# Attention in a hybrid decoder layer: values as the weights of a half-width product, two token tiles streamed, sums divided behind it

## The chip, the core and the metric

The kernel runs on one core of a Trainium2 chip. The metric is device time in microseconds for one execution. A core has five engines that work from queues of their own, in order: TensorE (PE, with its weight loads shown apart as PEld), VectorE (DVE), ScalarE (ACT), GpSimd (POOL) and SyncE (SP), which here issues most DMAs. Products land in PSUM, eight banks of 2 KB on each of 128 partitions; the other engines read them from there. Everything else lives in SBUF or DRAM.

## What is computed

One decoder layer on 1024 tokens of width 1024, float32. The part that matters here is the attention group, 8 heads of 64, and what follows it:

```python
z = h @ W_in                       # q, k, v of the attention, and the RWKV group's columns
# A: causal dilated window attention, branches (128,1), (512,4), (2048,16);
#    the branches share their scores, so that each key has a weight 0 to 3
#    num = sum_j count(t,j) exp(s_tj) v_j ;  den = sum_j count(t,j) exp(s_tj)
attn  = rms_norm(num / den, attn_out_gain)
rw    = rwkv7(...)                 # the recurrent group, R
mixed = concatenate([attn, rw]) @ w_out
x = x + rms_norm(mixed, norm_mix_post)
x = x + rms_norm(relu(rms_norm(x) @ w_ffn_up)**2 @ w_ffn_down)
```

The number of branches in which a key takes part is put into the scores as a logarithm, from a table `strip` that depends on the distance alone.

## The kernel before

The stages follow one another: norm of x and its transposes, the projections with the recurrent part (up to about 446 us), attention (462 to 637), the mixing with `w_out` (to about 758), and the two products of the feed-forward part, each by a Strassen-like scheme of seven products. Most products are fp32r with high and low parts (`mm3`, three products); `mm` with plain float32 operands leaves two records in the trace.

**Attention** (`attn_pair`, L837) goes over four pairs of heads, a pair holding two heads in 64 partitions each. For each head, `qr` is loaded twice into the two halves of the partitions (L842), GpSimd makes `qs` from it, rounded to fp32r and scaled (L844), and VectorE puts the remainder into the lower half (L845); so one product over 128 rows takes high and low part at once. `kr` is loaded in the same way (L850), GpSimd rounds it to `kh` (L853), VectorE forms the rest `kl` (L854). The raw tiles, `qs`, `kh` and `kl` have two buffers each, one for each head of a pair, so that the next pair's can be made when the present pair's last readers are done. `vT` is transposed by TensorE into `Vt` (L863), keys on the partitions.

Then eight tiles of 128 queries, i = 0 to 7, in two groups of four (`qg`). For a tile and a head the scores `pS` of all keys up to the diagonal are formed in banks of up to 512 columns (L888). VectorE adds the table and takes the minimum in one instruction (L890); ScalarE makes the exponential and its row sum `den` (L893). TensorE transposes the 128x128 blocks into `pT` (L900), and ScalarE (first bank) or VectorE (second bank) copies them into `PT` (L902, L904), keys on the partitions. The product `av` (L869 to L872) takes each block of `PT` as the weights and streams the 64 columns of the head's values:

```python
mm(po[:, ii, h], PTs[h][:, j], Vt[:, j, h * 64:h * 64 + 64], j == 0, j == i)
```

Its output has queries on the partitions, so the division by the row sum is one VectorE product with the reciprocal (L910, L912). It is emitted one tile late (`pend`). `ao` goes to DRAM as rows (`a_d`, L914); its squares are summed over the columns (L917, L918) for the RMS norm.

The order of the instructions of an engine comes from a scheduler that goes by the priority under which they were written. Attention is written with a high priority (L936, L1049); what remains of the projections (`rest`, the last pair's q, k and v), the loading of `w_out` (`load_wo`) and R's first products fill the gaps. In the recurrent part and, from L1078 on, in the mixing, TensorE's order is the written one (`manual_schedule`).

**The mixing** takes the token tiles in the order 0, 4, 1, 5, 2, 6, 3, 7. `half_a` (L975) loads 128 rows of `a_d`, scales them by the attention's RMS factor `sa[:, 1]` on ScalarE, transposes them (`half_t`, L961) and splits them into high and low part; `half_r` does the same without scale for R's rows. `half_mm` multiplies a half with four blocks of `w_out`, 24 products of 512 columns into `pm`. For the first two tiles R's half is done during the attention and kept in SBUF (`part`); R's half of the third is bound to come behind the last `av` (L1062). `mix_x1` (L988) adds the halves if they are apart, forms the squares and the norm and adds x.

The squares' sums `sq4` become `sa` by one reduction and the `rsqrt` chain on VectorE (L1064 to L1066).

## Time and profile before

| what | value |
|---|---|
| time, median of three runs | 1360.32 us (1360.21 to 1365.02) |
| the profiled execution | 1361.23 us; its span 1359.4 us |
| TensorE's granted clock, mean over the span | 0.991 |
| stage up to 70 us: length, PE, DVE, ACT busy | 70, 54.3, 54.8, 49.4 us |
| 70 to 446, projections and recurrence | 376, 362.1, 231.2, 149.8 us |
| 637 to 758, the mixing | 121, 114.7, 97.9, 69.6 us |
| 758 to 1056, up product | 298, 296.8, 218.0, 124.1 us |
| 1056 to the end, down product | 304, 292.8, 194.4, 123.3 us |

The span is the time from the first to the last instruction of the program; some 1.8 us of the execution lie around it. Busy time is the union of an engine's instructions. A matmul's record lasts until its last result is written, and records overlap, so that the price of one in a burst is read from the distance between the starts, not from its duration. In rows of the timeline the columns are start, length, engine, line, operation, output and inputs, weights' shape, streamed shape and count; neighbouring equal instructions are merged into one row. In rows of groups the columns are count, busy us, mean ns of one, and the idle time of the engine just before them with what ended it.

### The profile page before, as it was taken

To read this page: it belongs to the slowest core of one execution; us is meant where nothing else is said; L and a number is where in the kernel's file an instruction comes from. 1 tells how busy PE (TensorE), PEld (TensorE's weight loads), DVE (VectorE), ACT (ScalarE), POOL (GpSimd) and SP (SyncE) were. 2 spreads that over 40 slices of the span, in tenths; PEclk is the share of its full clock that TensorE was granted. 3 is DMA by queue.
4 is the path that set the end of the run, shared out by engine and by line. 5 is a ranking of instruction groups with operands and counts; after the bars stand their busy time and mean duration, and the time that the engine had idled before them with its cause. 6 is when DMAs were issued, how large, how long until landed. Compare 5 with 4: busy or idle time off the path is not lost.

```text
span 1359.4 us, 22401 instructions
## 1 busy us (share of the span) xinstructions
PE 1307.3 (96%) x8784; PEld 1086.4 (80%) x8784; DVE 914.7 (67%) x1647; ACT 625.0 (46%) x1026; POOL 44.7 (3%) x56
## 2 busy tenths in 40 slices
PE   6999999999999999999998999999999999999997
PEld 5777887788777798988887888888887888888885
DVE  7867658531678567655788986677766786445686
ACT  7652324233555367654656444343434344443442
POOL 0000000000000100110000000000000002000110
PEclk9999999899999999999999999999999999999999
DMA  7346746676685656321434344444366995346564
GB/s 255 114 170 163 194 125 179 184 206 204 182 248 145 194 145 181 102 55 38 138 121 139 132 168 152 168 153 150 132 209 217 322 349 172 95 139 200 186 215 157
DMA packets 161193, 231.02 MB, mean 170 GB/s; under 512 B 51680, under 2 KB 88800, under 8 KB 161088
## 3 DMA queue, kind: packets, MB, share of 16 engines
q1 hardware_dynamic: 153024, 208.62, 48.8%
q10 hardware_dynamic: 8064, 20.98, 4.6%
q8 instruction: 69, 1.13, 0.4%
q14 instruction: 36, 0.29, 0.1%
HBM read 156.66 MB, written 72.89 MB: 169 GB/s over the span
## 4 chain that ended last, share of the span: by engine, by line
PE 77%; DVE 11%; DMA 5%; ACT 4%; issue 2%; SPq 0%; POOL 0%; DVEq 0%; ACTq 0%; POOLq 0%
PE X L47 12%; PE dX L47 9%; PE Z L47 6%; PE pm L47 5%; PE dZ L47 5%; PE po L47 5%; PE dY L47 3%; PE z_av L47 3%; PE z_k L47 3%; PE Y L47 3%; PE pS L47 3%; PE z_v L47 3%; PE z_aq L47 2%; PE pT L900 2%; PE z_r L47 2%
## 5 line engine op out<-in xcount | busy, mean ns | idle before, releaser
L47 PE MATMUL dX<-wow,wou 128*128 128x512 f32 x768 | 176.6, 390 | 3.3 <-ACT wow L1106 1.8
L47 PEld LDWEIGHTS dX<-wow,wou 128*128 128x128 f32 x768 | 143.6, 188 | 35.6 <-DVE wow L1107 3.4
L47 PE MATMUL dZ<-wow,wou 128*128 128x512 f32 x384 | 87.4, 389 | 0.0
L47 PEld LDWEIGHTS dZ<-wow,wou 128*128 128x128 f32 x384 | 72.1, 188 | 14.9
L1106 ACT ACTIVATE wow<-wd 128x1024 fp32r<-128x1024 f32 x40 | 42.3, 1059 | 87.1 <-PE dZ L47 29.8
L1107 DVE TENSOR_TENSOR wou<-ur,wou 128x1024 fp32r<-128x1024 f32 x56 | 72.0, 1288 | 10.8 <-ACT wou L1106 10.5
L47 PEld LDWEIGHTS po<-Vt,PT 128*128 128x128 f32 x576 | 72.6, 191 | 4.8 <-ACT PT L902 2.2
L47 PE MATMUL po<-Vt,PT 128*128 128x64 f32 x576 | 74.0, 269 | 0.7 <-ACT PT L902 0.4
L1107 DVE TENSOR_TENSOR wow<-wd,wow 128x1024 fp32r<-128x1024 f32 x40 | 49.9, 1251 | 36.3 <-ACT wow L1106 35.8
L1106 ACT ACTIVATE wou<-ur 128x1024 fp32r<-128x1024 f32 x56 | 58.6, 1049 | 26.2 <-DMA ur<-u_d 18.8
L893 ACT ACTIVATE S<-S,mn 128x128 f32<-128x128 f32 (+7 forms) x64 | 49.4, 774 | 20.8 <-DVE mn L890 20.7
L890 DVE CUSTOM_DVE_ANT_0 S<-pS,stripT 128x512 f32<-128x512 f32 (+3 forms) x64 | 37.4, 590 | 26.1 <-PE pS L47 15.9
L1193 ACT ACTIVATE r<-u 128x512 f32<-128x512 f32 x48 | 30.1, 627 | 48.4 <-DVE u L1191 48.1
L47 PE MATMUL z_aq<-hT,wh_aq 128*128 128x512 f32 x128 | 47.3, 424 | 3.5 <-DVE ev_v L192 3.5
L47 PE MATMUL pm<-WO,mxr 128*128 128x512 f32 x192 | 48.6, 398 | 0.0
L902 ACT ACTIVATE PT<-pT 128x512 f32<-128x512 f32 (+3 forms) x64 | 32.9, 515 | 32.2 <-PE pT L900 30.2
L1107 DVE TENSOR_TENSOR wow<-TK,wow 128x1024 fp32r<-128x1024 f32 x16 | 20.8, 1301 | 38.9 <-ACT wow L1106 38.9
L47 PE MATMUL Z<-HB,wo 128*128 128x512 f32 x192 | 46.1, 389 | 0.0
L47 PE MATMUL pm<-WO,mxa 128*128 128x512 f32 x192 | 45.8, 394 | 0.0
L900 PE MATMUL pT<-cst,S 128*128 128x128 f32 x288 | 44.4, 276 | 1.0 <-DVE rden L910 0.5
L47 PE MATMUL X<-HB,wo 128*128 128x512 f32 x180 | 43.6, 390 | 1.6 <-ACT HB L1029 1.6
L47 PE MATMUL z_k<-hT,wh_k 128*128 128x512 f32 x128 | 43.2, 398 | 1.7 <-DVE z L223 1.4
(388 smaller groups left out, 3102.5 us busy)
## 6 DMA issues: line engine op xcount, KB each, us to landing
ur<-u_d SPq DMA_DIRECT2D x56, 512.0 KB, 4.2
wd<-in_wdown_dram SPq DMA_DIRECT2D x40, 512.0 KB, 3.9
u_d<-S SPq DMA_DIRECT2D x64, 256.0 KB, 2.1
u_d<-u SPq DMA_DIRECT2D x48, 256.0 KB, 2.1
wr_upa<-in_wup_dram SPq DMA_DIRECT2D x16, 512.0 KB, 3.8
wr_upb<-in_wup_dram SPq DMA_DIRECT2D x16, 512.0 KB, 3.8
TK<-in_wdown_dram SPq DMA_DIRECT2D x16, 512.0 KB, 7.3
x<-in_x_dram SPq DMA_DIRECT2D x8, 512.0 KB, 6.0
```

The source lines that it names most:

```text
L47: return PE.matmul(o, lhsT, rhs, start=start, stop=stop, skip_group_check=True)
L890: V.tensor_tensor_reduce(Sx[:, lo:hi], pS[:, :hi - lo], stripT[:, so:so + hi - lo], 1.0, 3e38 if k == 0 else mn[:, 0:1], OP.add, OP.min, a ...
L893: A.activation(Sx[:, :w], Sx[:, :w], AF.Exp, scale=-1.0, bias=mn[:, nbk - 1:nbk], accum_out=den[:, i, h:h + 1])
L900: PE.transpose(pt[:, j], Sx[:, (4 * k + j) * P:(4 * k + j + 1) * P], ident)
L902: A.activation(PT[:, 0:nb_], pt[:, 0:nb_], AF.Copy)
L1106: A.activation(w[:, 0, 0:n], raw, AF.Copy)
L1107: E.tensor_tensor(w[:, 1, 0:n], raw, w[:, 0, 0:n].bitcast(F32), OP.subtract)
L1193: A.activation(r, src, AF.Relu)
```

## The change

The product of probabilities and values is turned round. The 64 columns of a head's values become the weights, and the transposed probabilities of two query tiles (i = 2g and 2g+1, 256 columns, the later tile first) are streamed. The output has the head's 64 columns on the partitions, the first head on 0 to 63 and the second on 64 to 127, and the tokens along the columns. The two heads' products alternate. There are four groups g for each pair in place of two; `PT` holds two tiles of a head, block by block.

Since the queries are no longer on the partitions, the row sums can't divide by a scalar for each partition. Their reciprocals `rden` are written to DRAM (`rd_d`), loaded back spread over 64 partitions for each head (`rb`), and `ao` is the product of `po` and `rb`. `a_d` holds the attention output transposed, and `half_a` loads what it needs without a transpose; it splits the unscaled values, and the RMS factor moves behind the product: R's part is multiplied by its inverse (`sa[:, 2]`) ahead of the transposes where both halves are accumulated together, and the sum is scaled afterwards (`joint`), or, for the first two tiles, the attention half alone where the halves are added. The squares are summed over the pairs in `sqa` and over the partitions by eight products with two columns, ones in either half (`pq`).

The scores are the same products, but written for both heads of a tile ahead of their exponentials; the score tiles `S` have two buffers of 512 columns and two of 1024. For tiles 0 to 3 the second head's blocks are copied by VectorE instead of ScalarE. `qs` and `kh` are made on ScalarE instead of GpSimd. The evacuated projections and `ao` share two buffers `ev` in the attention's pool; before, the projections had three in a pool of their own. R's half of the third tile is no longer done behind the last `av` but in the mixing's loop.

The diff, without what the functions above show as removed:

```diff
-        a_d = dp.tile([S, 512], F32, name="a_d")
+        a_d = dp.tile([P, 4, S], F32, name="a_d")
+        rd_d = dp.tile([4, 4, 2, 2, P], F32, name="rd_d")
...
-                zt_ = evp.tile([P, 512], F32, name=f"ev_{nm}_{hf}", tag="ev" if i >= 8 else "kr", bufs=3 if i >= 8 else 8)
+                zt_ = evp.tile([P, 512], F32, name=f"ev_{nm}_{hf}", tag="ev" if i >= 8 else "kr", bufs=evb[0] if i >= 8 else 8)
...
-        ev_ctx = tc.tile_pool(name="ev2", bufs=2)
-        evp = ev_ctx.__enter__()
...
-        ap_ = at_ctx.__enter__()
-        sq4 = cp.tile([P, 4, 8], F32, name="sq4")
-        sa = cp.tile([P, 5, 8], F32, name="sa")[:, 0:2]
+        ap_ = evp = at_ctx.__enter__()
+        evb[0] = 2
+        sa = cp.tile([P, 9, 8], F32, name="sa")[:, 0:4]
         stripT = ap_.tile([P, S], F32, name="stripT", bufs=1)
+        sqa = ap_.tile([P, S], F32, name="sqa", bufs=1)
...
-                G.tensor_scalar(qs, qr, -0.125, 0.0, op0=OP.mult, op1=OP.add)
+                A.activation(qs, qr, AF.Copy, scale=-0.125)
...
-                gcopy(kh, kr)
+                A.activation(kh, kr, AF.Copy)
...
-            den = sm.tile([P, 8, 2], F32, name=f"den{p}", tag="den")
-            rden = sm.tile([P, 8, 2], F32, name=f"rden{p}", tag="rden")
...
+            def av(g, PTs, rb):
...
+                po = ps.tile([P, 512], F32, name=f"po{p}_{g}", tag="by"[g % 2], bufs=1)[:, 0:256]
+                for j in [0, 2 * g + 1] + list(range(1, 2 * g + 1)):
+                    n = 128 if j > 2 * g else 256
+                    for h in range(2):
+                        last_av[0] = mm(po[own[h], 0:n], Vt[:, j, h * 64:h * 64 + 64], PTs[h][:, 256 * j:256 * j + n], j == 0, j == 2 * g or g == 0)
+                cols = slice(256 * g, 256 * g + 256)
+                ao = ap_.tile([P, 512], F32, name=f"ao{p}_{g}", tag="ev")[:, 0:256]
+                V.tensor_tensor(ao, po, rb, OP.mult)
+                nc.sync.dma_start(a_d[:, p, cols], ao)
+                if p == 0:
+                    A.activation(sqa[:, cols], ao, AF.Square)
+                else:
+                    sq = ap_.tile([P, 256], F32, name=f"sqa{p}_{g}", tag="sq", bufs=1)
+                    A.activation(sq, ao, AF.Square)
+                    V.tensor_tensor(sqa[:, cols], sqa[:, cols], sq, OP.add)
...
             pend = []
...
-            def av(po, i, ii, PTs):
-                for h in range(2):
-                    for j in range(i + 1):
-                        last_av[0] = mm(po[:, ii, h], PTs[h][:, j], Vt[:, j, h * 64:h * 64 + 64], j == 0, j == i)
...
+            for g in range(4):
+                PTs = [ap_.tile([P, 1920 if g % 2 else 1408], F32, name=f"PT{p}_{g}_{h}", tag=f"PT{g % 2}") for h in range(2)]
+                den = sm.tile([P, 8, 2], F32, name=f"den{p}_{g}", tag="den")[:, 0:2]
+                for i in (2 * g, 2 * g + 1):
                     w = P * (i + 1)
...
+                    nbk = 1 if w <= 512 else 2
+                    Sx = [ap_.tile([P, 512 * nbk], F32, name=f"S{p}_{i}_{h}", tag=f"S{nbk}") for h in range(2)]
+                    mn = [sm.tile([P, 2], F32, name=f"mn{p}_{i}_{h}", tag="mn", bufs=4) for h in range(2)]
+                    for k in range(nbk):
+                        lo_, hi_ = 512 * k, min(w, 512 * k + 512)
+                        so = S - w + lo_
+                        pS = [ps.tile([P, 512], F32, name=f"pS{p}_{i}_{h}_{k}", tag="w") for h in range(2)]
+                        for h in range(2):
+                            for q in range(2):
+                                mm(pS[h][:, :hi_ - lo_], QS[h][:, i * P:(i + 1) * P], (KH, KL)[q][h][:, lo_:hi_], q == 0, q == 1)
+                        for h in range(2):
+                            V.tensor_tensor_reduce(Sx[h][:, lo_:hi_], pS[h][:, :hi_ - lo_], stripT[:, so:so + hi_ - lo_], 1.0,
+                                                   3e38 if k == 0 else mn[h][:, 0:1], OP.add, OP.min,
+                                                   accum_out=mn[h][:, k:k + 1])
                     for h in range(2):
...
+                        A.activation(Sx[h][:, :w], Sx[h][:, :w], AF.Exp, scale=-1.0, bias=mn[h][:, nbk - 1:nbk],
+                                     accum_out=den[:, h, 1 - i % 2:2 - i % 2])
+                        o = P * (2 * g + 1 - i)
                         for k in range(nbk):
                             nb_ = min(4, i + 1 - 4 * k)
                             pt = ps.tile([P, 4, P], F32, name=f"pT{p}_{i}_{h}_{k}", tag="ac"[k], bufs=1)
                             for j in range(nb_):
...
+                                PE.transpose(pt[:, j], Sx[h][:, (4 * k + j) * P:(4 * k + j + 1) * P], ident)
+                            f = (4 * k + nb_ - 1) * 256 + o
+                            dst = PTs[h][:, 4 * k * 256 + o:f + P] if nb_ == 1 else PTs[h].rearrange("p (j c) -> p j c", c=P)[:, (4 * k * 256 + o) // P:f // P + 1:2]
+                            if k == 0 and (h == 0 or nbk == 2):
+                                A.activation(dst, pt[:, 0:nb_], AF.Copy)
                             else:
...
+                                V.tensor_copy(dst, pt[:, 0:nb_])
+                    if i % 2 == 0 and pend:
+                        av(*pend.pop(0))
+                rden = sm.tile([P, 8, 2], F32, name=f"rden{p}_{g}", tag="rden")[:, 0:2]
+                V.reciprocal(rden, den)
+                nc.sync.dma_start(rd_d[p, g].rearrange("h s q -> q h s"), rden)
+                rb = ap_.tile([P, 256], F32, name=f"rb{p}_{g}", tag="rb", bufs=1)
+                for h in range(2):
+                    nc.sync.dma_start(rb[own[h]], rd_d[p, g, h:h + 1].rearrange("o s q -> o (s q)").to_broadcast([64, 256]))
+                pend.append((g, PTs, rb))
+            av(*pend.pop(0))
...
+        def half_r(t, tag, scaled=True):
+            m = w2p.tile([P, 512], F32, name=f"mr{t}", tag="mr", bufs=1)
+            nc.sync.dma_start(m, r_d[t * P:(t + 1) * P, :])
+            if scaled:
+                A.activation(m, m, AF.Copy, scale=sa[:, 2, t:t + 1])
+            pt = ps.tile([P, 4, P], F32, name=f"mxtr{t}", tag=tag, bufs=2 if tag in "zw" else 1)
             for j in range(4):
                 PE.transpose(pt[:, j], m[:, j * P:(j + 1) * P], ident)
...
+            mx = stg.tile([P, 2, 4, P], F32R, name=f"mxr{t}", tag="wh")
             A.activation(mx[:, 0], pt, AF.Copy)
             V.tensor_tensor(mx[:, 1], pt, mx[:, 0].bitcast(F32), OP.subtract)
             return mx
...
-            m = w2p.tile([P, 512], F32, name=f"mr{t}", tag="mr", bufs=1)
-            nc.sync.dma_start(m, r_d[t * P:(t + 1) * P, :])
...
-        def half_a(t, tag):
-            m = mp.tile([P, 512], F32, name=f"ma{t}", tag="ma")
-            nc.sync.dma_start(m, a_d[t * P:(t + 1) * P, :])
-            A.activation(m, m, AF.Copy, scale=sa[:, 1, t:t + 1])
...
+        def half_a(t):
+            m = mp.tile([P, 4, P], F32, name=f"ma{t}", tag="ma")
+            nc.sync.dma_start(m, a_d[:, :, (t ^ 1) * P:(t ^ 1) * P + P])
+            mx = stg.tile([P, 2, 4, P], F32R, name=f"mxa{t}", tag="wl")
+            A.activation(mx[:, 0], m, AF.Copy)
+            V.tensor_tensor(mx[:, 1], m, mx[:, 0].bitcast(F32), OP.subtract)
+            return mx
...
-            if y is None:
+            joint = y is None
+            if joint:
...
-                    V.tensor_tensor(src[n], src[n], pm[n], OP.add)
+                    V.scalar_tensor_tensor(src[n], pm[n], sa[:, 1, t:t + 1], src[n], OP.mult, OP.add)
...
+            if joint:
+                V.tensor_tensor(st[:, 2:3], st[:, 2:3], sa[:, 3, t:t + 1], OP.mult)
...
+            if joint:
+                V.tensor_tensor(st[:, 4:5], st[:, 4:5], sa[:, 1, t:t + 1], OP.mult)
...
-        rx, part, pms = {0: half_r(ORD[0], "z"), 1: half_r(ORD[1], "z")}, {}, {}
...
+        rx, part, pms = {0: half_r(ORD[0], "z", False), 1: half_r(ORD[1], "z", False)}, {}, {}
         for i in range(2):
             pr_ = pm_new(ORD[i], "zz")
             half_mm(ORD[i], pr_, rx.pop(i), 4, True, True)
             part[i] = mp.tile([P, D], F32, name=f"y{ORD[i]}", tag="y")
             for n in range(2):
                 A.activation(part[i][:, n * 512:n * 512 + 512], pr_[n], AF.Copy)
-            if i == 0:
-                rx[2] = half_r(ORD[2], "z")
-        pms[2] = pm_new(ORD[2], "zz")
-        with tc.issue_after(last_av[0].ins):
-            half_mm(ORD[2], pms[2], rx.pop(2), 4, True, False)
-        V.tensor_reduce(sa[:, 0, :], sq4.rearrange("q p t -> q t p"), axis=AX.X, op=OP.add)
+        pq = ps.tile([P, 8, 2], F32, name="pq", tag="a", bufs=1)
+        for t in range(8):
+            mm(pq[:, t ^ 1], sqa[:, t * P:(t + 1) * P], bone)
+        V.tensor_reduce(sa[:, 0, :], pq, axis=AX.X, op=OP.add)
         V.tensor_scalar(sa[:, 0, :], sa[:, 0, :], 1.0 / 512, NORM_EPS, op0=OP.mult, op1=OP.add)
         rsqrt(sa[:, 1, :], sa[:, 0, :], 8, "a", "wa")
+        V.tensor_tensor(sa[:, 2, :], sa[:, 0, :], sa[:, 1, :], OP.mult)
+        V.tensor_tensor(sa[:, 3, :], sa[:, 1, :], sa[:, 1, :], OP.mult)
...
-        ax = {0: half_a(ORD[0], "a")}
+        ax = {0: half_a(ORD[0])}
...
-                ax[i + 1] = half_a(ORD[i + 1], "a")
+                ax[i + 1] = half_a(ORD[i + 1])
...
-            if 2 < i + 1 < 8:
+            if 1 < i + 1 < 8:
...
-            if 2 < i + 2 < 8:
-                rx[i + 2] = half_r(ORD[i + 2], "b")
+            if 1 < i + 2 < 8:
+                rx[i + 2] = half_r(ORD[i + 2], "a")
```

46 lines of the change are left out of this document (1 added, 45 removed).

## The prediction

> **What bounds the kernel now.** I read the page first, then the windows of the attention section, then the groups of lines inside it, then single stretches of the timeline. The page gives the span and each engine's share.
>
> ```profile
> span 1359.4 us, 22401 instructions
> PE 1307.3 (96%) x8784; PEld 1086.4 (80%) x8784; DVE 914.7 (67%) x1647; ACT 625.0 (46%) x1026; POOL 44.7 (3%) x56
> ```
>
> TensorE is the long engine of the whole kernel, so the first question is whether it is in the changed section too. The windows answer that (start:end, length, then busy us of each engine). Attention runs from the first `qs` at 462 to the last product at 637.
>
> ```profile
> 462.00:637.00 175.00, 170.68 (x1228) 151.90 (x1226) 107.12 (x272) 102.01 (x224) 17.29 (x16) 1.00 0.42 118
> 585.00:597.00 12.00, 11.99 (x89) 10.91 (x89) 7.48 (x13) 4.54 (x8) 4.57 (x4) 1.00 0.37 89
> 597.00:637.00 40.00, 37.75 (x283) 33.27 (x282) 21.18 (x64) 23.10 (x53) 0.00 (x0) 1.00 0.11 34
> 637.00:646.00 9.00, 7.51 (x39) 5.92 (x38) 4.30 (x16) 2.85 (x5) 0.00 (x0) 1.00 0.32 89
> ```
>
> TensorE is busy for 170.7 of 175 us at a granted clock of 1.00; VectorE and ScalarE work 107 and 102. The third row is the pair without filler from other stages: 37.75 of 40. So attention is TensorE's, and a microsecond taken off it counts until VectorE or ScalarE is the longer one. What they and TensorE do there (busy, mean ns):
>
> ```profile
> L47 PE MATMUL po<-Vt,PT 128*128 128x64 f32 x576 | 74.0, 269 | 0.7 <-ACT PT L902 0.4 <-ACT Vt L864 0.2
> ...
> L893 ACT ACTIVATE S<-S,mn 128x128 f32<-128x128 f32 (+7 forms) x64 | 49.4, 774 | 20.8 <-DVE mn L890 20.7
> ...
> L890 DVE CUSTOM_DVE_ANT_0 S<-pS,stripT 128x512 f32<-128x512 f32 (+3 forms) x64 | 37.4, 590 | 26.1 <-PE pS L47 15.9 <-PE pT L900 7.1 <-ACT S L893 1.7
> ...
> L902 ACT ACTIVATE PT<-pT 128x512 f32<-128x512 f32 (+3 forms) x64 | 32.9, 515 | 32.2 <-PE pT L900 30.2 <-PE pS L47 1.8
> ...
> L890 DVE CUSTOM_DVE_ANT_0 S<-pS,stripT,mn 128x128 f32<-128x128 f32 (+3 forms) x32 | 17.5, 548 | 2.9 <-PE pS L47 2.0
> L904 DVE COPY PT<-pT 128x128 f32<-128x128 f32 (+3 forms) x32 | 15.7, 490 | 17.9 <-PE pT L900 17.8
> L893 ACT ACTIVATION_READ_ACCUMULATOR S<-S,mn 128x1 f32 x64 | 12.2, 191 | 0.0
> ...
> L845 DVE SCALAR_TENSOR_TENSOR qs<-qr,qs 64x1024 fp32r<-64x1024 f32 x8 | 9.8, 1222 | 3.5 <-POOL qs L844 3.4
> L854 DVE TENSOR_TENSOR kl<-kr,kh 128x1024 fp32r<-128x1024 f32 x8 | 9.8, 1220 | 5.0 <-POOL kh L122 4.9
> ...
> L890 DVE DVE_READ_ACCUMULATOR2_ANT mn<- 128x1 f32 x96 | 8.0, 84 | 0.0
> ...
> L912 DVE TENSOR_TENSOR ao<-po,rden 128x512 f32<-128x512 f32 x8 | 5.5, 691 | 7.8 <-PE po L47 7.8
> L918 DVE TENSOR_REDUCE sq<-sqa 128x4 f32<-128x512 f32 x8 | 5.5, 685 | 1.4 <-ACT sqa L917 1.4
> ...
> L917 ACT ACTIVATE sqa<-ao 128x512 f32<-128x512 f32 x8 | 5.0, 629 | 10.1 <-DVE ao L912 10.1
> ...
> L932 ACT ACTIVATE WO<-wo 128x1024 fp32r<-128x1024 f32 x2 | 2.1, 1048 | 0.0
> ...
> L910 DVE RECIPROCAL rden<-den 128x8 f32<-128x8 f32 x8 | 1.6, 199 | 4.1 <-ACT S L893 4.1
> ```
>
> The first row is the product that is rewritten, the dearest TensorE group here. ScalarE and VectorE mostly wait for scores and transposes, that is for TensorE.
>
> **The product itself.** The timeline shows its price. A long burst of `po`, and three bursts from the recurrent part, whose weights are 64 columns wide and whose outputs alternate between the two halves of the partitions, as the changed product's will:
>
> ```profile
> 342.41 0.40 PE L47 MATMUL z_aq<-hT,wl_aq 128*128 128x512 f32 x1
> 342.65 0.39 PE L47 MATMUL z_aq<-hT,wh_aq 128*128 128x512 f32 x1
> 342.96 1.15 PE L47 MATMUL O<-VU,TR 128*64 128x64 f32 x32
> 344.05 1.09 PE L47 MATMUL E<-TR,Zp 64*64 64x128 f32 x16
> 345.07 1.16 PE L47 MATMUL p<-AR,K 64*128 64x128 f32 x16
> ```
>
> ```profile
> 633.77 3.68 PE L47 MATMUL po<-Vt,PT 128*128 128x64 f32 x32
> 637.26 5.71 PE L47 MATMUL pm<-WO,mxr 128*128 128x512 f32 x24
> ...
> 651.10 0.60 PE L964 MATMUL mxta<-cst,ma 128*128 128x128 f32 x4
> 651.46 5.74 PE L47 MATMUL pm<-WO,mxa 128*128 128x512 f32 x24
> ```
>
> ```profile
> 81.62 1.84 PE L47 MATMUL pst<-cst,sq 128*128 128x2 f32 x16
> ```
>
> Each plain f32 product leaves two records. The `po` burst streams 32 x 64 = 2048 columns and holds TensorE from 633.77 to 637.26, 3.49 us: 109 ns a record. That isn't streaming: `pst` streams 2 columns a record and needs 1.84/16 = 115 ns as well. Both change 128x128 weights every record. `O` streams the same 2048 columns in 1.09 us, and `E`, with twice the columns a record and half the records, in 1.02. So with alternating halves the price goes by columns, about 1.05 us for 2048, one change of array layout included.
>
> Before: 576 x 64 = 36,864 columns, 18 x 3.49 = 62.8 us. After: for a pair and head there are (1+3+5+7) blocks of 256 columns and 4 of 128, 4608 columns; 8 such, two records each, 73,728 columns in 320 records. That is twice the columns, since half of the array's width is used: 36 x 1.02 to 1.09 = 36.7 to 39.2, I take 37.8. **Gain 25.0 us of TensorE's time.**
>
> The Trainium skill ("TensorEngine Tiling (Array Packing)", Tiling Modes, Key Properties) speaks against it: changing the tiling mode drains the TensorE. The trace agrees that a change costs: `z_aq` to `O` takes 0.31 us where `z_aq` to `z_aq` takes 0.24. By that rule the sum depends on how often the product is interrupted, which is the third rival below.
>
> **What VectorE and ScalarE get.** Two more shapes, from the same view with the forms kept apart:
>
> ```profile
> L904 DVE COPY PT<-pT 128x256 f32<-128x256 f32 x8 | 3.4, 424 | 2.7 <-PE pT L900 2.7
> ...
> L902 ACT ACTIVATE PT<-pT 128x256 f32<-128x256 f32 x8 | 3.1, 384 | 0.6 <-PE pT L900 0.5
> ```
>
> VectorE now: 37.4+17.5+8.0+15.7+9.8+9.8+5.5+5.5+1.6 = 110.8, or 27.7 a pair. Added: 16 transposed blocks (second head, tiles 0 to 3) at 0.49 = 7.8; 16 `ao` of 256 columns at 0.424 = 6.8 for 5.5; 12 adds to `sqa`, at most 0.424 each, 5.1 for the reductions' 5.5; eight more reciprocals, 1.6. That makes 121.1, **30.3 a pair**. ScalarE now: 49.4+12.2+32.9+5.0 = 99.5. Added: 16 conversions of `qs` and `kh` taken from GpSimd at 1.05 (as L932) = 16.8; squares 16 x 0.384 = 6.1 for 5.0; less 16 copies at 0.515 = 8.2. That makes 109.2, **27.3 a pair**. TensorE for a pair without filler: 37.75 - 25/4 = 31.5. So it stays the longest, by one microsecond a pair. Three engines near 30 in a dependent chain will not all stay full: I give back **2.5 us** for waits inside the pairs (bounds 0 and 6, the 6 being about 4% of the section).
>
> **Between the pairs.** The next pair's operands start when its predecessor's last scores have been formed, because `qs` has two buffers:
>
> ```profile
> 462.30 1.05 POOL L844 TENSOR_SCALAR qs<-qr 128x1024 fp32r<-128x1024 f32 x1 [201.25 <-DVE wl_av L712]
> ```
>
> ```profile
> 585.29 1.04 POOL L844 TENSOR_SCALAR qs<-qr 128x1024 fp32r<-128x1024 f32 x1 [31.70 <-PE pS L47]
> ...
> 592.69 1.04 POOL L122 TENSOR_SCALAR kh<-kr 128x1024 fp32r<-128x1024 f32 x1 [3.92 <-DMA kr<-zs_d]
> 594.90 1.04 POOL L122 TENSOR_SCALAR kh<-kr 128x1024 fp32r<-128x1024 f32 x1 [1.17 <-DMA kr<-zs_d]
> ```
>
> A pair takes (585.29 - 462.30)/3 = 41.0 us. From `qs` at 585.29 to the second `kh`'s end at 595.94 pass 10.65 us: conversion, split, load of `kr` (two buffers `raw`), conversion. The change keeps these loads and moves the conversions into ScalarE's queue, where they wait for the last scores with exponentials and copies behind them, and those have TensorE's transposes behind them. Before, the 10.65 us were covered on TensorE by the old pair's products and filler (11.99 of 12 busy). After, the old pair leaves the last scores (4 x 0.24 = 1.0), 16 transposes (at `mxta`'s 0.09, 1.4) and the last group's product (7680 columns, 3.9): 6.3, or 4.3 uncovered. Three boundaries make 13. The independent filler, products with `WO` and the last projections, covers part; the 24 of one `WO` half take 5.7 us, and two halves are free to be placed. I give back **5 us** (bounds 0 and 13).
>
> **The divisor's detour.** The sums' reciprocals go to DRAM and return twice broadcast (one write, two loads in SP's queue, behind nothing long). No row shows 4-byte writes; the nearest are
>
> ```profile
> a_d<-ao SPq DMA_DIRECT2D x8, 256.0 KB, 2.3
> ma<-a_d SPq DMA_DIRECT2D x8, 256.0 KB, 2.7
> ```
>
> so about 2.3 + 2.7 + 0.2 for the reciprocal = 5.2 us, at least; much smaller transfers can hardly be faster than half of it. The next tile and the group's own product stand between; a tile is about 30.3/8 = 3.8 us. I put nothing more on it here; if the cover is gone it is the first rival.
>
> **The end of the section and the mixing.** Before, 24 `pm` products (5.71 us) cover the chain from the last `ao` to the scaled attention half. After, no attention half waits for the RMS scale, but the eight `pq` sums stand in TensorE's queue ahead of the first one, and wait for the last `ao`, its square and the add: about 0.4 + 0.4 + 0.4 and hops. I give back **1 us** (0 to 3). In the mixing 32 `mxta` transposes go (4 in 0.36, so 2.9) and 16 records of `pq` at 0.115 (1.8) come: **gain 1.1**. The scale of R's rows on ScalarE (6) replaces that of A's (8), one iteration ahead: no price; if that cover went, the third row's kind of wait, under 1 us each. The shared `ev` buffers delay projections only: nothing.
>
> Sum: -25.0 + 2.5 + 5 + 1 - 1.1 = -17.6. The profiled execution took 1361.2 (span 1359.4 and 1.8 around), 0.9 over the median 1360.3. **Forecast: 1360.3 - 17.6 = 1342.7.**
>
> **Rivals.** *The divisor comes late (slower).* `ao` stands in VectorE's in-order queue ahead of the next scores; where the detour's 5.2 us outlast what lies between, VectorE stands and then all do. For: the early tiles are short, half of the mean or 1.9 us, so 3.3 are uncovered there; against: scheduling may put `ao` later. At 3.3 for two groups of each pair and 1.4 for the third that is 4 x 8.0 = 32 instead of 2.5: 1372. It decides the sign from 1.7 us a group over twelve groups. *The halves don't run together*, because something stands between two heads' products: 73,728 columns at double price, 75.6 us, 37.8 more than forecast: 1380. Against: `O` and `E`. *The layout changes too often.* Priced at 0.07 to enter and as much or a little more to leave, 0.17 together; 80 interruptions instead of 36 are +7.5: 1350. *Boundaries stay bare*: 13 instead of 5 and 6 instead of 2.5, +11.5: 1354, about no change. *All is covered*: neither loss, 1335, and without layout changes (36 x 0.17) 1329.
>
> **How the numbers follow.** About 0.5% (6.8 us) is what can be told from no change here. Forecast, 1337 to 1349: 0.46. All covered: 0.16. Too many layout changes or half-bare boundaries, to 1353.5: 0.14. Within 0.5%: 0.13. Late divisor 0.07, halves apart 0.04. So faster 0.76, same 0.13, slower 0.11; the range 1330 to 1358 leaves out about 0.04 below and 0.15 above.
>
> **What would show it.** Right: `po` with 320 records and 36 to 40 us from its bursts' starts, two records nearly together; first `qs` of two pairs some 36 to 37 us apart; TensorE still over 90% busy. Wrong: `po` streaming at 200 ns a record; VectorE's `ao` rows with idle time ended by a DMA into `rb` of over 10 us; TensorE idle at boundaries for over 4 us each; gaps ahead of `pq` beyond 3 us.

## The result and the profile after

| | before | after |
|---|---|---|
| median of the runs | 1362.61 us (1360.21 to 1365.02, 4 runs) | 1489.02 us (1486.84 to 1491.8, 4 runs) |
| ratio, 95% interval | | 1.0929 [1.0895, 1.0962] |
| span of the profiled execution | 1359.4 us | 1485.0 us |
| granted clock of TensorE, mean | 0.991 | 0.95 |

The kernel became 126 us slower; forecast were 18 us less, and the range ended at 1358. The page of the kernel after, its first lines, the slices of the granted clock and the group of the final multiplication:

```profile
span 1485.0 us, 21981 instructions
...
PE 1335.1 (90%) x8512; PEld 1066.8 (72%) x8512; DVE 923.1 (62%) x1697; ACT 636.3 (43%) x1032; POOL 27.4 (2%) x40
...
PEclk9999999999998888888779999999999999999999
...
L878 DVE TENSOR_TENSOR ao<-po,rb 128x256 f32<-128x256 f32 x16 | 6.8, 423 | 68.8 <-DMA rb<-rd_d 61.2
```

No engine has become long: TensorE's share fell from 96% to 90%. Sixteen instructions that compute for 6.8 us have 68.8 us of idle time ahead of them, 61.2 of it ended by the loads of `rb`. So the loss is waiting, and the slices of the clock say where: from the thirteenth to the twenty-first, 445 to 780 us, which is attention. Its window (length, busy us of PE, PEld, DVE, ACT, POOL, clock, DMA share, GB/s), from the first `qs` to behind the last `ao`:

```profile
462.00:765.00 303.00, 204.69 (x1012) 137.97 (x1010) 118.44 (x314) 117.66 (x237) 0.00 (x0) 0.81 0.41 80
```

The 175 us of before have become some 300, which is the whole difference. TensorE is busy for 205 of 303 us, at a lower clock than before (0.81 for 1.00). VectorE (118.4) and ScalarE (117.7) are near the sums that the prediction made for them (121.1 and 109.2), and far from full. What TensorE waits for, by groups in 460 to 760 us (busy, mean ns, idle before it):

```profile
L47 PE MATMUL po<-PT,Vt 128*64 128x256 f32 (+1 forms) x320 | 54.8, 402 | 7.8 <-ACT PT L919 7.4
L915 PE MATMUL pT<-cst,S 128*128 128x128 f32 x288 | 52.5, 314 | 22.3 <-DVE PT L921 9.3 <-ACT S L908 7.4 <-ACT sqa L881 4.6
L47 PE MATMUL pS<-kh,qs 128*128 128x512 f32 (+3 forms) x96 | 45.1, 476 | 42.7 <-DVE mn L904 27.8 <-ACT kh L856 14.7
...
L866 PE MATMUL vt<-cst,vT 128*128 128x128 f32 x32 | 7.7, 398 | 10.9 <-DMA vT<-zs_d 10.9
```

The rewritten product itself waits for little. The scores wait for VectorE (27.8), whose `mn` rows stand behind `ao`. They also wait for the conversions of the next pair's operands (14.7), and the transposes `vt` for a load (10.9). VectorE's queue in the last group of the last pair, and SyncE's queue beside it:

```profile
748.02 0.18 DVE L925 RECIPROCAL rden<-den 128x4 f32<-128x4 f32 x1 [1.37 <-ACT S L908]
...
762.77 0.42 DVE L878 TENSOR_TENSOR ao<-po,rb 128x256 f32<-128x256 f32 x1 [11.18 <-DMA rb<-rd_d]
```

```profile
748.23 0.38 SPq L926 DMA_DIRECT2D rd_d<-rden  x1
750.75 0.53 SPq L988 DMA_DIRECT2D ma<-a_d  x1
758.59 2.12 SPq L929 DMA_DIRECT2D rb<-rd_d  x2
763.22 0.33 SPq L879 DMA_DIRECT2D a_d<-ao  x1
```

From the reciprocal's end at 748.20 to `ao` at 762.77 pass 14.6 us; the prediction had put the detour at 5.2. None of the sixteen groups took less than 13.0 us for it. The write is issued at 748.23, and the two loads that need it only at 758.59. SyncE issues one load meanwhile and then stands still, with everything behind it in its queue. The table of the DMAs (KB each, us from issue to landing) and SyncE's waits in the window:

```profile
vT<-zs_d SPq DMA_DIRECT2D x4, 512.0 KB, 9.7
rb<-rd_d SPq DMA_DIRECT2D x32, 64.0 KB, 3.4
...
rd_d<-rden SPq DMA_DIRECT2D x16, 2.0 KB, 10.4
```

```profile
SPq L929 <- DMA rd_d<-rden: 88.9, 11, 11.6
```

A write of 2 KB takes 10.4 us, more than the loads of 64 and 512 KB in the same table. And the load `vT` of 512 KB takes 9.7 us where it took 3.4 before:

```profile
vT<-zs_d SPq DMA_DIRECT2D x4, 512.0 KB, 3.4
```

### The profile page after: what moved, and what is told of

Read it like the earlier page. It is cut to its first block, busy times and chain, and to the rows that moved or that the text cites. A ratio compares the mean times of both kernels' runs of the same rounds, so it can differ in the third digit from the quotient of the medians.

```text
span 1485.0 us, 21981 instructions
## 1 busy us (share of the span) xinstructions
PE 1335.1 (90%) x8512; PEld 1066.8 (72%) x8512; DVE 923.1 (62%) x1697; ACT 636.3 (43%) x1032; POOL 27.4 (2%) x40
## 4 chain that ended last, share of the span: by engine, by line
PE 62%; DMA 17%; DVE 14%; ACT 3%; issue 3%; SPq 1%; DVEq 0%; ACTq 0%
PE X L47 11%; PE dX L47 7%; PE Z L47 6%; PE pm L47 5%; DMA rd_d<-rden 5%; PE dZ L47 4%; PE dY L47 3%; PE z_v L47 3%; PE Y L47 3%; PE z_k L47 2%; PE z_aq L47 2%; DMA bv<-v_d 2%; PE z_ak L47 2%; PE z_r L47 2%; PE qu L47 2%
## 5 line engine op out<-in xcount | busy, mean ns | idle before, releaser
L47 PE MATMUL pS<-kh,qs 128*128 128x512 f32 (+3 forms) x96 | 45.1, 476 | 42.7 <-DVE mn L904 27.8
L915 PE MATMUL pT<-cst,S 128*128 128x128 f32 x288 | 52.5, 314 | 22.3 <-DVE PT L921 9.3
L1125 ACT ACTIVATE wou<-ur 128x1024 fp32r<-128x1024 f32 x56 | 58.5, 1049 | 21.6 <-DMA ur<-u_d 14.2
L915 PEld LDWEIGHTS pT<-cst,S 128*128 128x128 f32 x288 | 39.0, 161 | 39.0 <-ACT S L908 13.0
L47 PEld LDWEIGHTS pS<-kh,qs 128*128 128x128 f32 x96 | 21.4, 226 | 61.1 <-DVE mn L904 34.9
L47 PE MATMUL po<-PT,Vt 128*64 128x256 f32 (+1 forms) x320 | 54.8, 402 | 7.8 <-ACT PT L919 7.4
L47 PE MATMUL pm<-WO,mxr 128*128 128x512 f32 x192 | 51.8, 412 | 0.0
L47 PE MATMUL pm<-WO,mxa 128*128 128x512 f32 x192 | 51.1, 422 | 0.0
L878 DVE TENSOR_TENSOR ao<-po,rb 128x256 f32<-128x256 f32 x16 | 6.8, 423 | 68.8 <-DMA rb<-rd_d 61.2
L921 DVE COPY PT<-pT 128x128 f32<-128x128 f32 (+3 forms) x48 | 23.5, 490 | 41.4 <-PE pT L915 40.7
```

The source lines that it names most:

```text
L47: return PE.matmul(o, lhsT, rhs, start=start, stop=stop, skip_group_check=True)
L878: V.tensor_tensor(ao, po, rb, OP.mult)
L915: PE.transpose(pt[:, j], Sx[h][:, (4 * k + j) * P:(4 * k + j + 1) * P], ident)
L921: V.tensor_copy(dst, pt[:, 0:nb_])
L1125: A.activation(w[:, 0, 0:n], raw, AF.Copy)
```

## The experiments

All are edits of the kernel after. "Before" is the run of the kernel before on the same chip. The first four are one execution each; the others have several, with an interval.

| run | what it is | us | before | ratio |
|---|---|---|---|---|
| e1 | no divisor | 1390.65 | 1363.08 | |
| e2 | divisor moved, not awaited | 1431.52 | 1363.08 | |
| e3 | divisor written in rows of 512 B | 1379.1 | 1363.08 | |
| e4 | divisor spread by TensorE | 1388.77 | 1363.08 | |
| e5 | e3, `ao` with buffers of its own | 1378.71 | 1362.14 | 1.0124 [1.0086, 1.0161] |
| e6 | e5, conversions on GpSimd | 1378.55 | 1362.14 | 1.0127 [1.0094, 1.0161] |
| e7 | e6, scores head by head | 1374.42 | 1362.14 | 1.0102 [1.0062, 1.0141] |
| e8 | e3, one head's products after the other's | 1405.58 | 1362.14 | 1.0325 [1.0281, 1.0369] |
| e9 | e7, product in whole bursts | 1368.88 | 1361.4 | 1.0046 [1.0031, 1.0061] |
| e10 | e7, 64 full-width instructions inside the product | 1406.69 | 1361.4 | 1.0340 [1.0313, 1.0368] |
| e11 | e7, 64 half-width instructions there | 1380.61 | 1361.4 | 1.0141 [1.0119, 1.0163] |
| e12 | e6, product in whole bursts | 1383.48 | 1361.2 | 1.0166 [1.0142, 1.0191] |

**e1, no divisor.** The write, the loads and the wait go; the division is left out.

```diff
-                nc.sync.dma_start(rd_d[p, g].rearrange("h s q -> q h s"), rden)
-                rb = ap_.tile([P, 256], F32, name=f"rb{p}_{g}", tag="rb", bufs=1)
-                for h in range(2):
-                    nc.sync.dma_start(rb[own[h]], rd_d[p, g, h:h + 1].rearrange("o s q -> o (s q)").to_broadcast([64, 256]))
+                rb = c[:, 0:256]
```

> The reciprocals neither go to DRAM nor come back; the products are multiplied by a table of constants that lies ready in SBUF, so the division by the row sums is left out. Theory (the write of the reciprocals in 4-byte pieces lands 10.4 us late, and VectorE's queue at the division and SyncE's queue at the loads stand behind it): nearly all of the 126 us go, the attention section (303 us, 462 to 765) takes 150 to 165 us, the kernel 1335 to 1355 us. Rival (the rest of the change costs it: conversions on ScalarE, scores of both heads ahead of the exponentials with two buffers, the half-width product with its changes of array layout, the shared evacuation buffers): the section stays above 230 us and the kernel above 1420 us.

Measured 1390.65, between the two. By this one run about 98 of the 126 us hang on the detour, and some 28 on something else.

**e2, the divisor moved but not awaited.** The transfers stay, `ao` multiplies by constants; the division is left out.

```diff
-                V.tensor_tensor(ao, po, rb, OP.mult)
+                V.tensor_tensor(ao, po, c[:, 0:256], OP.mult)
```

> The reciprocals still go to DRAM and are loaded back spread, but the products are multiplied by a table of constants, so that VectorE waits for no load (the division is left out). It parts the theory in two. If the time is in VectorE's wait ahead of the division (68.8 us of idle time there), the kernel falls to 1345 to 1370 us. If it is in what stands behind the write in SyncE's queue and in the transfers issued after it (88.9 us of SyncE's waits), it stays at 1430 to 1480 us. I expect both to count: about 1400 us. The rival of the first run would have it near 1480 us.

Measured 1431.52: 41 us over e1 with nobody waiting for the result, and 57 under the kernel after. The first part goes with what the write does to its queue. SyncE's wait at the loads `rb` in e2, 455 to 765 us, and the other engines' waits in 455 to 720 us:

```profile
SPq L929 <- DMA rd_d<-rden: 119.0, 16, 10.1
...
DVE kl L857 <- ACT kh L856: 30.2, 7, 7.9
ACT kh L856 <- DMA kr<-zs_d: 28.1, 6, 7.2
...
PE pS L47 <- ACT kh L856: 24.9, 6, 6.2
```

SyncE stands still in each of the sixteen groups. The next pair's keys `kr` come late, `kh` behind them, the split `kl` and the scores behind that. The other 57 us go with VectorE's wait at `ao`, the one thing that e2 takes away.

**e3, the same bytes in rows.** TensorE transposes the 128 x 4 reciprocals, and the write has 4 pieces of 512 B in place of 512 pieces of 4 B. Loads, waits and order in the code are the change's.

```diff
-                nc.sync.dma_start(rd_d[p, g].rearrange("h s q -> q h s"), rden)
+                pr4 = ps.tile([P, 512], F32, name=f"pr4{p}_{g}", tag="c", bufs=1)[0:4, 0:P]
+                PE.transpose(pr4, rden.rearrange("p h s -> p (h s)"), ident)
+                rr = ap_.tile([P, P], F32, name=f"rr{p}_{g}", tag="rr", bufs=1)[0:4]
+                V.tensor_copy(rr, pr4)
+                nc.sync.dma_start(rd_d[p, g].rearrange("h s q -> (h s) q"), rr)
```

> The detour stays whole, but TensorE first turns the 128 x 4 reciprocals into 4 rows of 128, VectorE copies them out of PSUM, and the write goes in 4 rows of 512 bytes in place of 512 pieces of 4 bytes. If the pieces make the write slow, its landing falls from 10.4 to 2 to 3 us, VectorE's idle time ahead of the division from 68.8 to under 25 us, and the kernel to 1360 to 1395 us. If the way through DRAM is slow whatever the shape, landing and time stay (above 1450 us).

Measured 1379.1: 110 us under the kernel after, with more instructions. SyncE's timeline for the last group, its waits, and VectorE's in e3:

```profile
651.59 0.27 SPq L930 DMA_DIRECT2D rd_d<-rr  x1
652.96 1.12 SPq L933 DMA_DIRECT2D rb<-rd_d  x2
```

```profile
SPq L933 <- DMA rd_d<-rr: 7.0, 7, 2.1
```

```profile
DVE ao L878 <- DMA rb<-rd_d: 5.6, 2, 4.6
```

From write to loads it is 1.4 us in place of 10.4, SyncE waits for the write 7.0 us in all in place of 88.9, and `ao` 5.6 in place of 61.2. So the cause is the pieces, 512 of 4 B in place of 4 of 512 B; their size and their number change together, and the runs don't part the two. The way through DRAM as such costs little here. The Trainium skill ("DMA: Bandwidth & Descriptors", Specifications) asks for at least 512 B a piece for line rate and says that below it the engine reads, modifies and writes. The runs agree on the side (10.4 us against 1.4); the page gives no price for 4 B.

That e3 is faster than e1, which does less, by 11.6 us, shows what such runs can't tell: each edit lets the scheduler place the attention work anew, which is the likely reason here, and a difference of 10 us between two of these kernels proves little. The 110 us are far above that, and e5 below, with four executions, stands where e3's one does.

**e4, no DRAM at all.** Four small products for each group spread the reciprocals over the partitions.

```diff
...
+                for s in range(2):
+                    for h in range(2):
+                        mm(pb[own[h], s * P:s * P + P], rden[:, h, s:s + 1].to_broadcast([P, 64]), ident)
+                rb = ap_.tile([P, 256], F32, name=f"rb{p}_{g}", tag="rb", bufs=1)
+                A.activation(rb, pb, AF.Copy)
...
-                nc.sync.dma_start(rd_d[p, g].rearrange("h s q -> q h s"), rden)
...
```

> The reciprocals don't leave the chip: TensorE spreads them over 64 partitions by four products for each group, the reciprocal repeated 64 times as weights and the identity streamed, into the free half of the product's PSUM bank; ScalarE copies the result to SBUF, VectorE multiplies as before. The whole computation is done. It adds 16 x 8 records of 128 columns, about 7 us of TensorE at the 0.055 us of the rows of before, and 16 x 0.4 us of ScalarE. Theory: 1340 to 1362 us, so at or below the kernel of before; rival: above 1420 us.

Measured 1388.77, a miss: no better than the way through DRAM in rows. So what is left doesn't look like the detour. Why e4 is 10 us slower than e3 stays open.

**e5, e6, e7: the change's other parts undone, one upon the other.** e5 on e3 (buffers):

```diff
-        evb[0] = 2
+        evb[0] = 1
...
-                ao = ap_.tile([P, 512], F32, name=f"ao{p}_{g}", tag="ev")[:, 0:256]
+                ao = ap_.tile([P, 256], F32, name=f"ao{p}_{g}", tag="ao")
```

> The run with the reciprocals written in rows, and besides the evacuated projections get a buffer of their own (one of 512 columns) while the products' output has two of 256: the same memory, but the last pair's projections no longer queue behind the first pair's four outputs. In that run TensorE's filler z stood still from 462 to about 523. If that is part of what remains (16 us over the kernel before), 6 to 12 us go: 1367 to 1373 us. If what remains sits in the attention's own chains, under 3 us go.

e6 on e5 (conversions of `qs` and `kh`):

```diff
-                A.activation(qs, qr, AF.Copy, scale=-0.125)
+                G.tensor_scalar(qs, qr, -0.125, 0.0, op0=OP.mult, op1=OP.add)
...
-                A.activation(kh, kr, AF.Copy)
+                gcopy(kh, kr)
```

> The run before this one, and qs and kh are made on GpSimd again as in the kernel of before: 16 conversions of 1.05 us leave ScalarE's queue. If the conversions stand among exponentials and copies and hold up the pairs' starts, 4 to 10 us go: 1360 to 1367 us. If ScalarE had room for them, within 3 us of the run before.

e7 on e6 (one head's scores and exponentials, then the other's, with three buffers `Sx` as before):

```diff
-                    Sx = [ap_.tile([P, 512 * nbk], F32, name=f"S{p}_{i}_{h}", tag=f"S{nbk}") for h in range(2)]
...
-                        for h in range(2):
-                            for q in range(2):
-                                mm(pS[h][:, :hi_ - lo_], QS[h][:, i * P:(i + 1) * P], (KH, KL)[q][h][:, lo_:hi_], q == 0, q == 1)
+                    for h in range(2):
+                        Sx = ap_.tile([P, S], F32, name=f"S{p}_{i}_{h}", tag="Sx", bufs=3)
...
+                            for q in range(2):
+                                mm(pS[:, :hi_ - lo_], QS[h][:, i * P:(i + 1) * P], (KH, KL)[q][h][:, lo_:hi_], q == 0, q == 1)
```

> The run before this one, and the scores are written head by head with three score buffers of 1024 columns, as in the kernel of before (the same memory as two of 512 and two of 1024). What is left of the change is the half-width product, the reciprocals' rows and the unscaled attention half. If the order of the scores with two buffers holds the chain of score, exponential and transpose, 5 to 15 us go and the kernel falls below the one of before: 1345 to 1360 us. If the half-width product itself is at fault, it stays above 1362 us.

Measured 1378.71, 1378.55 and 1374.42. The first two give nothing. The third gives about 4 us, which the intervals don't tell from nothing, as they overlap. After all three, the kernel is still 12 us over before. So most of that lies in what they leave in place: the half-width product, the rows of reciprocals, or the unscaled attention half with what it needs in the mixing.

**e8, do the halves run together?** On e3, all products of one head of a group, then all of the other's, so that neighbours use the same half.

```diff
-                for j in [0, 2 * g + 1] + list(range(1, 2 * g + 1)):
-                    n = 128 if j > 2 * g else 256
-                    for h in range(2):
+                for h in range(2):
+                    for j in [0, 2 * g + 1] + list(range(1, 2 * g + 1)):
+                        n = 128 if j > 2 * g else 256
```

> The run with the reciprocals written in rows, but the product takes all blocks of the first head and then all of the second, so that neighbouring products use the same half of the array. If the halves run together only when they alternate, the 320 records take about 0.21 us in place of 0.105, about 30 us more of TensorE, and the kernel 1395 to 1412 us (some of it into idle time). If alternation doesn't matter, it stays at 1379 us.

Measured 1405.58, 26 us over e3. The last burst of the section, of 26 records, in e3 and then in e8 (start, us, and the start of the next line; in both, 24 records stream 256 columns and 2 stream 128, and the line shows the shape of the first):

```profile
651.17 3.02 PE L47 MATMUL po<-PT,Vt 128*64 128x128 f32 x26
...
654.13 2.11 PE L47 MATMUL pm<-WO,mxa 128*128 128x512 f32 x8
```

```profile
669.37 4.80 PE L47 MATMUL po<-PT,Vt 128*64 128x256 f32 x26
674.10 1.50 PE L47 MATMUL pq<-cst,sqa 128*128 128x2 f32 x12
```

2.96 us against 4.73, or 114 ns a record against 182. In the change's order the two halves' records do overlap; the second rival is out.

**e9, whole bursts.** In e7's program the product is cut into 57 bursts by scores, transposes and projections that the scheduler sets between. Here it goes ahead of them: 27 bursts.

```diff
+                with tc.high_priority(offset=4000):
                     for j in [0, 2 * g + 1] + list(range(1, 2 * g + 1)):
...
```

> e7 with the products of values and probabilities of a group put ahead of the scores, transposes and projections that stand ready, so that TensorE runs them in 27 bursts in place of 57 (counted in the program). Theory (each interruption of a half-width burst costs about 0.3 us on top of its records, so that the 57 bursts gave back about half of the product's saving): 30 bursts fewer by 0.3 us, 9 us, less what the group's own waits take: 1363 to 1369 us, about the time of the kernel before. Rival (the 12 us that e7 still lacks lie in waits at the boundaries and in the mixing, not in the changes of width): within 3 us of e7, 1371 to 1378, or above.

**e10 and e11, the price of an interruption.** e10 puts a full-width transpose of a constant behind each step of the product but one in each group (the last; in the first group, the first of two), e11 a half-width product of a constant in the same 64 places. They write into the product's own PSUM bank, and the product's values do not stay right; only the times are read.

```diff
...
+                    if j != 2 * g:
+                        PE.transpose(pf[:, 256:384], ident, ident)
```

```diff
...
+                    if j != 2 * g:
+                        mm(pf[own[0], 256:384], ident[:, 0:64], ident, True, True)
```

> e7 with one full-width transpose of a constant, into unused columns of the same PSUM bank, behind each step of the product but the last: 64 instructions more, which depend on nothing, up to 64 interruptions more. Theory (an interruption costs about 0.3 us beside the record of some 0.1 us): 64 x 0.3 + 64 x 0.1 = 26 us over e7, about 1400. Rival (only the records cost): 64 x 0.1 = 6 us over e7, about 1381.

> The control to e10: the same 64 places hold a half-width product of a constant (64 columns of weights, 128 columns streamed), so the width never changes. Both theories: only its records, 64 x some 0.1 to 0.2 us, 6 to 13 us over e7: 1381 to 1387. If e10 and e11 come out alike, the change of width costs nothing here, and an added instruction of either kind costs the same.

Measured: e9 1368.88 (5.5 us under e7), e10 1406.69 (32.3 over e7) and e11 1380.61 (6.2 over e7). The first is at the upper end of what was expected, the second some 7 us above it, the third at the lower end. The 5.5 and 6.2 us are too small to prove much alone, as said of e3. But 64 added instructions cost 6 us where the width stays, and 32 where it changes. Some of e10's fell where the product was cut already: in the traces e10 has 112 half-width bursts and e11 has 62. So 26 us go with 50 more changes of width and back, about 0.5 each; what the scheduler placed anew may be part of that. TensorE's timeline in e10 shows some by themselves:

```profile
665.67 1.03 PE L916 MATMUL pT<-cst,S 128*128 128x128 f32 x8
666.46 1.17 PE L47 MATMUL pm<-WO,mxa 128*128 128x512 f32 x4
...
673.54 0.65 PE L47 MATMUL po<-PT,Vt 128*64 128x256 f32 x4
674.12 0.33 PE L878 MATMUL po<-cst 128*128 128x128 f32 x1
674.38 0.65 PE L47 MATMUL po<-PT,Vt 128*64 128x256 f32 x4
674.97 0.33 PE L878 MATMUL po<-cst 128*128 128x128 f32 x1
675.22 0.65 PE L47 MATMUL po<-PT,Vt 128*64 128x256 f32 x4
```

Four half-width records and one wide one take 0.84 us (673.54 to 674.38). In e9 a burst of 30 half-width records stands undisturbed:

```profile
637.08 3.45 PE L47 MATMUL po<-PT,Vt 128*64 128x256 f32 x30
640.46 0.27 PE L926 MATMUL pr<-cst,rden 128*4 128x128 f32 x1
```

That is 3.38 us, 113 ns a record, so four take 0.45. A wide transpose among its like takes 0.10 (eight from 665.67 to 666.46). What is left of 0.84 is 0.29 us for one change of width and back. In e11 the same step, four records of the product and two of the constant, takes 0.65 us (654.51 to 655.16), or 108 ns a record: nothing is left there. The rest of the 26 us that e10 loses to e11, beyond 50 times 0.29 or 14.5, isn't accounted for.

**e12, whole bursts with the change's order of scores.** e9's edit on e6 in place of e7.

> e9 (bursts kept whole) with the change's own order of scores again: those of both heads ahead of their exponentials, so that while one head's exponential runs, TensorE has the other head's scores (e9's profile: the transposes wait 7.0 us for exponentials between 462 and 736 us, where the kernel before has none listed). 29 bursts in place of e9's 27. Theory (what e9 still lacks is work to cover the exponentials, which the interruptions had given by accident): the 7.0 us go, 1361 to 1366 us. Rival (the order of the scores costs as much as it gives, as from e6 to e7, where it was 4 us dearer): 1366 to 1374.

Measured 1383.48: 14.6 us over e9, above the rival's range too. The order that was to cover the exponentials makes the kernel slower. TensorE's window in e9 and in e12, and e12's waits in 455 to 655 us:

```profile
466.00:641.00 175.00, 162.73 (x998) 113.56 (x996) 118.00 (x325) 98.26 (x217) 19.30 (x16) 0.97 0.43 132
```

```profile
463.00:654.00 191.00, 170.00 (x1009) 116.54 (x1008) 119.27 (x324) 98.58 (x217) 18.42 (x16) 0.96 0.40 122
```

```profile
PE pT L916 <- ACT S L909: 5.8, 6, 2.2
PE pS L47 <- DVE mn L905: 5.8, 7, 2.1
PE mxtr L985 <- DMA mr<-r_d: 3.4, 1, 3.4
```

The exponentials are waited for as before (5.8 against e9's 7.0, below), and the scores now wait for `mn` as well (5.8 against 1.5). e12's window is 16 us longer; TensorE's idle time makes 8.7 of them (21.0 for 12.3), and 7.3 are more busy time, which these waits don't explain. Of the three parts undone in e5 to e7, the order of the scores is the only one seen to cost, and clearly so only once the bursts are whole.

**What e9 still lacks.** It is 0.46% over the kernel before [0.31, 0.61], a small loss, but one that the interval keeps apart from none. Its attention window is as long as that of before, 175 us. TensorE does 162.7 us of work in it where it did 170.7, so 8 us are saved, and 8 more are idle. Its waits in e9, 455 to 655 us, and in before, 455 to 640 us:

```profile
PE pT L914 <- ACT S L907: 7.0, 5, 3.6
PE mxtr L983 <- ACT mr L980: 3.6, 1, 3.6
PE pq L47 <- DVE sqa L886: 2.7, 1, 2.7
PE pT L914 <- DVE PT L920: 1.8, 4, 0.8
PE pS L47 <- DVE mn L904: 1.5, 4, 0.6
```

```profile
PE pS L47 <- DVE kl L854: 1.7, 2, 0.9
PE pS L47 <- DVE mn L890: 0.5, 1, 0.5
PE pT L900 <- DVE rden L910: 0.5, 1, 0.5
PE pS L47 <- POOL kh L122: 0.4, 1, 0.4
```

No kernel of this study beats the one before.

## Why the prediction was wrong, point by point

**The step that failed** is "The divisor's detour": "so about 2.3 + 2.7 + 0.2 for the reciprocal = 5.2 us, at least; much smaller transfers can hardly be faster than half of it", and then "I put nothing more on it here". The price was taken over from a write of 256 KB for one of 2 KB, as if fewer bytes could not take longer. The trace has 10.4 us for the write and 14.6 for the whole way in the last group. A tile was put at 3.8 us and the longest product at 3.9, so even with both between, `ao` had to wait. The diff showed the 4-byte pieces and the prediction named them, but bounded their cost from below alone. With no row near it, the term needed a high upper bound. Its own sign of being wrong came: `ao` with idle time ended by a load of `rb`, 11.18 us in the row above.

**The first rival** named the mechanism (`ao` in VectorE's queue ahead of the next scores) at 1372 and 0.07. By e2 it was about half of it: 57 us by the wait, 41 by SyncE, which the prediction passed with "behind nothing long". Who stands behind a slow transfer in that queue, the next pair's `kr` and `vT`, wasn't asked.

**The product's gain of 25.0 us**: right inside a burst, and too high in whole. The forecast for 320 records was 36.7 to 39.2 us; at e9's 113 ns they take 36.2. Added up in the traces, from each burst's start to the start of what follows it, the product holds TensorE for 60.4 us in the kernel before, 51.4 in the kernel after (at its lower clock) and 42.4 in e9. So the gain was 9 us in the kernel after, and 18 in e9.

**The layout changes** were mis-sized: 0.17 us each and 36 of them, 6 us inside the product's price. e10's timeline has 0.29, and the program of the kernel after 50 bursts, which makes 14.5 us (e7's 57, 16.5): 8 us of the gain, where the third rival had 7.5 by more interruptions at the low price. e9's 27 bursts give a lower price: 42.4 less 36.2, or 0.23 each. The rule of the Trainium skill that the prediction weighed, the drain at a change of the tiling mode ("TensorEngine Tiling (Array Packing)", Key Properties), agrees with e10 against e11, 26 us for 50 more changes; it gives no figure.

**Waits in pairs and bare boundaries**, 2.5 + 5 + 1 = 8.5 us: in e9 dearer, and partly elsewhere. The five longest waits listed for e9 make 16.6 us, the four for before 3.1; the prediction's bounds for these terms reached to 22. The dependent chain in the pairs (7.0 us for exponentials) and the sums `pq` (2.7) were foreseen. The scale of R's rows, put at no price and under 1 us at worst, has one wait of 3.6. The bare boundaries don't show in e9, where the conversions are on GpSimd again; in the kernel after the scores wait 14.7 us for `kh`, and ScalarE, which makes it, 14.2 us for the late `kr`.

**VectorE and ScalarE**: the sums were about right (118 for 121, 118 for 109, in windows that hold some other work too), and neither became the bound. The conversions on ScalarE, priced by their cover at the boundaries, cost nothing that e6 could measure. "The shared `ev` buffers delay projections only: nothing": e5 agrees. The order of the scores had no price at all; it costs 4 us that can't be told from nothing (e6 to e7), or 14.6 (e12 to e9), depending on what else is placed.

**The share of each cause**, by runs: the pieces of 4 B 110 us (after to e3); then the order of the scores and the cut bursts about 10 (e5 and e6 at 1378.6 to e9). Between e9 and before lie 7 us: the work saved in attention is spent there on idle time, so the 7 lie outside that window. In the profiled executions, 8 us apart, half lies ahead of it (the first `qs` starts at 466.07 for 462.30) and half behind it (726.4 us for 722.4), where the mixing runs at a granted clock of 0.94 for 0.99. Which of them the change causes, and which are the scheduler's other order, stays open.

## What to carry to other kernels

Look at the size and the number of a small DMA's contiguous pieces, not at its bytes, and ask who stands behind it in its queue, before calling it hidden; a transpose that turns columns into rows of 512 B cost next to nothing beside that. A half-width product is as cheap as its stream only while it isn't interrupted, so count the bursts in the order that the scheduler really makes. And when TensorE gets a part for less, look for the work that was hidden behind it: here exponentials, RMS sums and scaled rows came to the surface for as much as was saved.

## What the runs showed of the hardware that wasn't expected

A DRAM write of 512 pieces of 4 B took 10.4 us from issue to landing, and the load `vT` in the same queue came late with it (9.7 us for 3.4). In the last group the trace shows where the time does not go. The write is issued at 748.23; 526 packets, all under 512 B, run between 749.1 and 749.5; from 749.5 to 752 there are two in all, on 16 DMA engines. Yet the loads that need the write are issued only at 758.59, and the load `ma`, issued at 750.75, lands after 10.2 us (3.2 in the median). So nine of the ten us pass after the pieces have been sent; what holds up their landing isn't shown. Where TensorE idles, its granted clock was lower too: 0.81 in the attention window of the kernel after, where the first scores' products have a mean of 476 ns for 401 in the kernel before. With 8 us more of idle time, in e9, it was 0.97. If the one causes the other, idle time is paid twice; no run separated them. And 64-column f32 products overlap two by two only when neighbours alternate the halves: 114 ns a record, and 182 when they don't.
